# The order of emission of a two-block kernel: 2.4 instead of 1.3 times the estimated latency for the steps of the RWKV7 recurrence

## The chip, the cores and the metric

The kernel runs on one core of a Trainium2 chip. The metric is the device time of one execution in microseconds (us). TensorE (PE), VectorE (DVE), ScalarE (ACT), GpSimd (POOL) and SyncE (SP, which issues the loads of the weights here) run in parallel, each through its own queue in order, and wait for each other by semaphores.

## What is computed

Two blocks run one after the other on one sequence of 256 tokens of width 1024, all in float32. Only the first block (two layers) is touched by the change:

```
for l in range(2):
    h = rmsnorm(x, norm_g[l])
    proj = h @ w_in[l]                          # 1024 x 18688
    y_a = hgrn2_mixer(...) * silu(a_g)          # 8 heads of 128, both directions
    y_b = retention_mixer(...) * silu(b_g)      # 8 heads, value width 256
    y_c = rwkv7_mixer(...) * silu(c_g)          # 16 heads of 64, both directions
    gates = sigmoid(merge)
    x = x + (gates0 * (y_a @ w_branch_a) + gates1 * (y_b @ w_branch_b)
             + gates2 * (y_c @ w_branch_c)) @ w_out
# rwkv7, for each token t and direction:
#   S = S * w_t + (S @ -kk_t) (kk_t * a_t)^T + v_t k_t^T;   o_t = S @ r_t
```

The second block (feed-forward layers, a short convolution, latent attention, attention to a memory) follows and stays as it is.

## The kernel before

Weights come in tiles of 128 x 1024 floats. Each is split into a high and a low part (ScalarE makes `whi`, L411, VectorE makes `wlo`, L412), and each product is made of three matmuls (L370 to L372, in `mm3`). A chunk is 1024 rows by 256 columns of a weight matrix: 16 pieces of three matmuls. The matmuls of a chunk write `pj` (projections), `pg` (gates of the merge), `pb` (branches) or `po` (output).

The work of a layer is written as five Python generators, and `weave` (L39) emits their instructions. Four are chains of dependent steps: `recurrences` (RWKV7: 8 pairs of heads, in chunks of 64 tokens), `heads` (4 pairs of HGRN2 heads, then 4 pairs of retention heads), `outs` and `operands` (before and after each pair of the recurrence). The fifth, `weights`, is the filler: projections, gates and branches, piece by piece. A chain's step yields (cost, latency) in estimated ns, a piece of weights yields 320, and either may yield a function: it is then left alone until the function says yes. `weave` keeps a clock, `now`. It takes the first chain whose due time has come, in the order recurrences, heads, outs, operands; if there is none it takes a piece of weights; and if the weights wait too, it moves the clock on to the next due time. After a step of a chain:

```
now += v[0]
ready[g] = now + scale[g] * v[1]
```

So `scale` (1.3 for recurrences, 1.35, 1.3 and 0.8 for the others) says how many times its estimated latency a step is allowed before the next step of its chain is due. The order of emission is the priority by which the compiler's scheduler orders the instructions of each engine among those that it holds to be ready; within a pool of tiles the buffers go round in the order of emission. `Ahead` (L94) moves the recurrence's instructions on VectorE, ScalarE and GpSimd 50 places up, and the splits of the weights go 80 up.

`recurrences` (L723) runs 9 rounds: `states(p-1)` and `prologue(p)` in step with each other (`in_step`, L69: costs are added, the larger latency counts). `prologue` is `rwkv_scores` (L982): a matmul for the bonus (L1009), scores (`psc`, L1021) into `SCa` and `SCr`, then an inverse by doubling, four times `pw` (L1081) and `px` (L1089) with VectorE work after each, and two last steps. `states` is `rwkv_states` (L1117): 10 steps of four small matmuls (`ch`, L1135, L1142, L1151) and then the outputs (`po`, L1169 and L1176). After it `("s", p)` is set.

The filler's order in `weights` (L746) is: HGRN2's inputs (4 times 5 chunks), retention's first pair (6), four gates of branch 0, a wait for the fourth pair of HGRN2 heads, branch 0 (4), retention's second and third pair (12), four gates of branch 1, branch 1's first half, retention's last pair, branch 1's second half, four gates of branch 2. What may be put in sooner by `spare` (L757) are the recurrence's own inputs k, v, r, g (4 chunks for every two pairs, in `NB` = 4 buffers, so each only when the fourth one before it has been used) and the gates of branch 0. HGRN2's and retention's inputs share a ring of five buffers (`ring`, L657). The gates of branch 1 share the buffers `SCr` with the recurrence's scores, and so they wait:

```
if tasks and (tasks[0][0] == 0 or ("s", 7) in ev):   # in spare
if b > 0:
    yield from until(("s", 7))                       # in gates
```

PSUM holds two banks for the filler's sums (`ps`). After `weave` come branch 2 (from all pairs of the recurrence) and the output projection, in plain order.

Of the kernel before, what the change touches and what calls it, by code (L numbers as in the profile page):

```python
# [29 lines left out]
def run(gen):  # L30

    try:
        while True:
            next(gen)
    except StopIteration as e:
        return e.value


def weave(chains, fill):  # L39

    scale = dict(chains)
    now, ready, wait, live = 0.0, {}, {}, list(scale) + [fill]
    while live:
        free = []
        for g in live:
            if g in wait and wait[g]():
                del wait[g]
                ready[g] = max(now, ready.get(g, 0.0))  # L50
            if g not in wait:
                free.append(g)
        g = next((g for g in free if g is not fill and ready.get(g, 0.0) <= now), None)
        if g is None:
            g = fill if fill in free else min(free, key=lambda g: ready.get(g, 0.0))
        now = max(now, ready.get(g, 0.0))
        v = next(g, None)
        if v is None:
            live.remove(g)
        elif callable(v):  # L60
            wait[g] = v
        elif g is fill:
            now += v
        else:
            now += v[0]
            ready[g] = now + scale[g] * v[1]


def in_step(gens):  # L69

    live, wait = list(gens), {}
    while live:
        took, later, moved = 0.0, 0.0, False
        for g in list(live):
            if g in wait and not wait[g]():
                continue
            wait.pop(g, None)
            v = next(g, None)
            while callable(v) and v():
                v = next(g, None)  # L80
            if v is None:
                live.remove(g)
            elif callable(v):
                wait[g] = v
            else:
                took, later, moved = took + v[0], max(later, v[1]), True
        if moved:
            yield took, later
        elif live:
            stuck = [wait[g] for g in live]  # L90
            yield lambda: any(w() for w in stuck)
# [430 lines left out]
class First(Core):  # L522
# [76 lines left out]
    def layer(s, l, then):  # L599
# [88 lines left out]
        def room():  # L688

            if due:  # L690
                n = 4 * due[0][0] + due[0][1] - NB
                return n < 0 or ("kvrg"[n % 4] + " used", 2 * (n // 4) + 1) in ev
            return True
# [8 lines left out]
        def operands():  # L702
            for p in range(8):
                for n in "kvr":
                    yield after((n, p // 2))
                if p > 0:
                    yield after(("bt", p - 1))
                yield from s.rwkv_operands(l, p, part("r", p), part("k", p), part("v", p), codes, ops)
                ev.add(("o", p))
                ev.add(("k used", p))  # L710
# [3 lines left out]
        def prologue(p):  # L714
            yield after(("o", p))
            pre[p] = yield from s.rwkv_scores(l, p, part("r", p), part("v", p), ops.pop(p), ev,
                                              lambda: p < 2 or ("g used", p - 2) in ev)

        def states(p):
            yield from s.rwkv_states(p, pre.pop(p), sts, lambda: p == 0 or ("g used", p - 1) in ev)  # L720
            ev.add(("s", p))

        def recurrences():  # L723

            for p in range(9):
                yield from in_step([states(p - 1)] * (p > 0) + [prologue(p)] * (p < 8))

        def outs():
            for p in range(8):
                yield after(("s", p))  # L730
                yield after(("g", p // 2))
                yield from s.rwkv_out(l, p, sts.pop(p), part("g", p))
                ev.add(("g used", p))

        def heads():
            st["ys"] = s.hs
            for j in range(4):
                yield lambda: ("h", j) in hin
                yield from s.hgrn_pair(l, j, hin["h", j], st["ys"], ev)
                ev.add(("h", j))  # L740
            for j in range(4):
                new = None if j % 2 else after(("a", ) if j == 0 else ("b", 0))
                yield from s.ret_pair(l, j, hin[("t", j)], st, new, ev)
                ev.add(("t", j))

        def weights():  # L746
            gate = lambda b, j: s.gate(l, b, j, st)

            def hproj(j):
                yield from s.hgrn_in(l, j, pj, pt, ring, hin)  # L750

            def rproj(j):
                yield from s.ret_in(l, j, pj, pt, ring, hin)

            tasks = [(b, gate(b, j)) for b in range(2) for j in range(4)]

            def spare():  # L757

                if due and room():
                    yield from rkv(*due.pop(0))  # L760
                    return True
                if tasks and (tasks[0][0] == 0 or ("s", 7) in ev):
                    yield from tasks.pop(0)[1]
                    return True
                return False

            def gates(b):
                if b > 0:
                    yield from until(("s", 7))
                while tasks and tasks[0][0] <= b:  # L770
                    yield from tasks.pop(0)[1]

            def until(*e):
                for i in e:
                    while i not in ev:
                        if not (yield from spare()):
                            yield after(i)

            def filled(g):

                for v in g:
                    while callable(v) and not v():
                        if not (yield from spare()):
                            yield v
                    if not callable(v):
                        yield v

            for j in range(4):
                yield from filled(hproj(j))
            yield from filled(rproj(0))  # L790
            yield from gates(0)
            yield from until(("h", 3))
            for j in range(4):
                yield from s.branch(l, 0, j, s.chunk(s.a["wba"][l][j]), st["ys"], st)
            ev.add(("a", ))
            yield from filled(rproj(1))
            yield from filled(rproj(2))
            yield from gates(1)
            for half in range(2):
                if half == 1:  # L800
                    yield from filled(rproj(3))
                yield from until(("t", 2 * half))
                for j in (0, 2):
                    b = [s.branch(l, 1, i, s.chunk(s.a["wbb"][l][i][2 * half:2 * half + 2]), st["ys"], st, True)
                         for i in (j, j + 1)]
                    for i in b:
                        for _ in range(8):
                            yield next(i)
                    yield after(("t", 2 * half + 1))
                    for i in b:  # L810
                        yield from i
                ev.add(("b", half))
            for j in range(4):
                yield from gate(2, j)
            while due:
                yield room
                yield from rkv(*due.pop(0))
# [15 lines left out]
        s.normed(s.x, y, s.P(f"ng{l}"), s.hb)  # L833
        if l == 0:
            nc.sync.dma_start(out=s.c1, in_=s.a["c1"])
        weave(((recurrences(), 1.3), (heads(), 1.35), (outs(), 1.3), (operands(), 0.8)), weights())
        run(out_c(0))
        run(out_c(1))
        mixed = st["gate", 0]
# [21 lines left out]
    def gate(s, l, b, j, st):  # L861

        if b == j == 0:
            st["gate", 0] = s.xp.tile([128, 8, T], F32, tag="x", name="gate")
        p = s.bank("pg")
        yield from s.fm(p, s.chunk(s.a["win"][l][MERGE + 4 * b + j]), s.hb)
        if b > 0 and j % 2 == 0:
            st["gate", b, j // 2] = s.rp.tile([128, 4, T], F32, tag="SCr", name="gate", bufs=2)
        s.nc.scalar.activation(s.gates(b, j, st), p, AF.Tanh, scale=0.5)
# [1035 lines left out]
```

## Time and profile before

| | us |
|---|---|
| median of 3 runs | 2739.27 (2730.82 to 2743.38) |
| the profiled execution | 2742.64 |
| its span, first to last instruction | 2740.8 |
| PE / DVE / ACT / POOL busy | 2636.6 / 2068.3 / 1494.7 / 283.6 |

The two layers of the first block take about 1690 us of the span: the first from the start to about 862 us, the second, with the same stretches, some 841 us later. Busy time is the time in which an engine worked on something; matmuls are pipelined, so a busy PE isn't PE at its peak. PEclk is the share of the full clock that TensorE was granted: 1.0 is 2.4 GHz, 0.5 is 1.2 GHz, and means lie between.

### The profile page before, as it was taken

How to read it: one execution, taken by the hardware profiler on the slowest of the kernel's cores; microseconds unless marked ns; L12 is line 12 of the kernel's file. 1: busy time of each engine (PE TensorE's matmuls, PEld its weight loads, DVE VectorE, ACT ScalarE, POOL GpSimd, SP SyncE). 2: the span in 40 equal slices, each digit the busy share in tenths (PEclk: the TensorE clock that was granted, in tenths of full speed). 3: DMA queues.
4: the chain of work that ended last, by engine and by line, in shares of the span. 5: the costliest groups of instructions: out<-in, count | busy, mean ns of one | idle time of the engine just before them, and what ended most of it. 6: DMA issues, size and time to landing. Idle time of an engine off the chain costs nothing.

```text
span 2740.8 us, 76128 instructions
## 1 busy us (share of the span) xinstructions
PE 2636.6 (96%) x31971; PEld 2499.4 (91%) x31971; DVE 2068.3 (75%) x4578; ACT 1494.7 (55%) x2968; POOL 283.6 (10%) x385
## 2 busy tenths in 40 slices
PE   7999999999999899999999999999999999999999
PEld 7888888899999888888799999999999999987999
DVE  8988889866668988898967677766776767756665
ACT  6665646444456665656444455555555555554554
POOL 1111112101021222212100111000000000000000
PEclk9998999999999999999999999999999999998999
DMA  5332222244556332223245555556455655542555
GB/s 178 111 105 75 98 76 83 94 150 151 179 171 197 112 106 84 93 80 100 73 133 163 173 165 197 184 171 187 151 181 182 185 180 163 170 132 76 173 182 161
DMA packets 111800, 385.38 MB, mean 141 GB/s; under 512 B 12384, under 2 KB 16992, under 8 KB 111200
## 3 DMA queue, kind: packets, MB, share of 16 engines
q1 hardware_dynamic: 111024, 379.86, 42.9%
q8 instruction: 251, 4.11, 0.6%
q10 hardware_dynamic: 432, 0.64, 0.1%
q14 instruction: 93, 0.76, 0.1%
HBM read 378.36 MB, written 2.10 MB: 139 GB/s over the span
## 4 chain that ended last, share of the span: by engine, by line
PE 76%; DVE 16%; ACT 3%; issue 2%; POOL 1%; DMA 1%; SPq 0%; ACTq 0%; DVEq 0%; POOLq 0%
PE pj L370 7%; PE pj L372 6%; PE pj L371 6%; PE pg L370 4%; PE pg L372 4%; PE pg L371 4%; DVE wlo L412 4%; PE pw L370 3%; PE pw L372 3%; PE pw L371 3%; PE pu L370 3%; PE pu L372 3%; PE pu L371 3%; PE pb L370 2%; PE pb L371 2%; PE pb L372 2%
## 5 line engine op out<-in xcount | busy, mean ns | idle before, releaser
L411 ACT CAST whi<-raw 128x512 fp32r<-128x512 f32 (+1 forms) x1407 | 862.0, 618 | 825.3 <-PE pj L372 228.0
L412 DVE TENSOR_TENSOR wlo<-raw,whi 128x512 fp32r<-128x512 f32 (+1 forms) x1407 | 984.8, 707 | 422.0 <-ACT whi L411 412.4
L370 PE MATMUL pj<-hb,wlo 128*128 128x256 f32 x1408 | 425.3, 302 | 7.5 <-DVE wlo L412 7.1
L372 PE MATMUL pj<-hb,whi 128*128 128x256 f32 x1408 | 405.0, 288 | 0.0
L371 PE MATMUL pj<-hb,whi 128*128 128x256 f32 x1408 | 404.3, 287 | 0.0
L370 PEld LDWEIGHTS pj<-hb,wlo 128*128 128x128 f32 x1408 | 271.4, 193 | 19.5 <-DVE wlo L412 6.7
L371 PEld LDWEIGHTS pj<-hb,whi 128*128 128x128 f32 x1408 | 271.9, 193 | 1.9 <-issue 0.2
L372 PEld LDWEIGHTS pj<-hb,whi 128*128 128x128 f32 x1408 | 271.6, 193 | 1.4 <-issue 0.2
L371 PE MATMUL pg<-hs,whi 128*128 128x256 f32 x704 | 200.3, 284 | 2.0 <-DVE hs L499 2.0
L370 PE MATMUL pg<-hs,wlo 128*128 128x256 f32 x704 | 200.2, 284 | 1.5 <-DVE x L518 1.5
L370 PE MATMUL pu<-hs,wlo 128*128 128x256 f32 x704 | 199.9, 284 | 1.8 <-DVE wlo L412 1.6
L370 PE MATMUL pw<-g,wlo 128*128 128x256 f32 x704 | 199.6, 284 | 0.7 <-DVE wlo L412 0.7
L372 PE MATMUL pg<-hs,whi 128*128 128x256 f32 x704 | 200.2, 284 | 0.0
L372 PE MATMUL pu<-hs,whi 128*128 128x256 f32 x704 | 199.6, 283 | 0.0
L371 PE MATMUL pu<-hs,whi 128*128 128x256 f32 x704 | 199.3, 283 | 0.0
L371 PE MATMUL pw<-g,whi 128*128 128x256 f32 x704 | 199.2, 283 | 0.0
L372 PE MATMUL pw<-g,whi 128*128 128x256 f32 x704 | 199.2, 283 | 0.0
L370 PE MATMUL pb<-hs,wlo 128*128 128x256 f32 x512 | 145.3, 284 | 0.0
L371 PE MATMUL pb<-hs,whi 128*128 128x256 f32 x512 | 144.6, 282 | 0.0
L372 PE MATMUL pb<-hs,whi 128*128 128x256 f32 x512 | 144.6, 282 | 0.0
L371 PEld LDWEIGHTS pg<-hs,whi 128*128 128x128 f32 x704 | 135.7, 193 | 2.2 <-DVE hs L499 2.2
L370 PEld LDWEIGHTS pu<-hs,wlo 128*128 128x128 f32 x704 | 135.0, 192 | 2.6 <-DVE wlo L412 2.4
(526 smaller groups left out, 6852.8 us busy)
## 6 DMA issues: line engine op xcount, KB each, us to landing
raw<-in_win SPq DMA_DIRECT2D x292, 512.0 KB, 3.6
raw<-in_w SPq DMA_DIRECT2D x256, 512.0 KB, 3.6
raw<-in_wbb SPq DMA_DIRECT2D x32, 512.0 KB, 3.6
raw<-in_wo SPq DMA_DIRECT2D x32, 512.0 KB, 3.5
raw<-in_wconv SPq DMA_DIRECT2D x20, 512.0 KB, 3.6
raw<-in_wba SPq DMA_DIRECT2D x16, 512.0 KB, 3.5
raw<-in_wbc SPq DMA_DIRECT2D x16, 512.0 KB, 3.5
raw<-in_lora SPq DMA_DIRECT2D x16, 256.0 KB, 2.6
```

What stands on the lines that cost most here:

```text
L370: mm(out=out, lhsT=al, rhs=bh, start=start, stop=False)
L371: mm(out=out, lhsT=ah, rhs=bl, start=False, stop=False)
L372: mm(out=out, lhsT=ah, rhs=bh, start=False, stop=stop)
L411: s.nc.scalar.copy(dh, src)
L412: (eng or s.nc.vector).tensor_tensor(dl, src, dh.bitcast(F32), ALU.subtract)
```

## The change

In `layer`, the number that goes with `recurrences()` in the call of `weave` becomes 2.4. Each step of the recurrence is then due 2.4 instead of 1.3 times its estimated latency after the one before it, in both layers. No instruction, buffer, wait or size is changed in the source; what changes is the place of instructions in the order of emission.

```diff
-        weave(((recurrences(), 1.3), (heads(), 1.35), (outs(), 1.3), (operands(), 0.8)), weights())
+        weave(((recurrences(), 2.4), (heads(), 1.35), (outs(), 1.3), (operands(), 0.8)), weights())
```

## Rows read from the trace of the kernel before

**Rows 1.** The page: busy time of each engine; the chain that ended last.

```profile
PE 2636.6 (96%) x31971; PEld 2499.4 (91%) x31971; DVE 2068.3 (75%) x4578; ACT 1494.7 (55%) x2968; POOL 283.6 (10%) x385
PE 76%; DVE 16%; ACT 3%; issue 2%; POOL 1%; DMA 1%; SPq 0%; ACTq 0%; DVEq 0%; POOLq 0%
```

**Rows 2.** Table of stretches: first layer's woven part, then two of the second layer.

```profile
core 0: us, PE busy (x) PEld busy (x) DVE busy (x) ACT busy (x) POOL busy (x), PEclk, DMA share, GB/s
46.80:541.00 494.20, 463.12 (x9031) 415.28 (x9030) 431.92 (x1092) 285.49 (x613) 88.29 (x142) 0.96 0.28 91
541.00:570.00 29.00, 29.00 (x283) 25.89 (x282) 15.86 (x42) 10.99 (x25) 0.73 (x1) 0.94 0.33 105
570.00:678.00 108.00, 107.39 (x855) 104.78 (x854) 77.20 (x150) 49.49 (x95) 11.11 (x12) 1.00 0.49 159
678.00:812.00 134.00, 133.76 (x1104) 132.55 (x1103) 89.62 (x144) 67.66 (x123) 19.94 (x14) 1.00 0.54 175
888.00:1383.00 495.00, 463.99 (x9082) 415.72 (x9081) 433.76 (x1102) 297.31 (x642) 100.75 (x150) 0.97 0.29 95
...
1412.00:1520.50 108.50, 107.89 (x866) 105.20 (x862) 76.90 (x149) 49.97 (x96) 10.82 (x12) 1.00 0.50 158
```

**Rows 3.** Waits of PE, 46.8 to 541 us.

```profile
engine line waited for: us in total, times, longest us
PE pw L1081 <- DVE XY L105: 5.3, 4, 2.0
PE pj L370 <- DVE wlo L412: 4.5, 4, 1.7
PE px L1089 <- DVE W L105: 2.8, 2, 1.9
```

**Rows 4.** Marks of order, first layer: duration ns min/median/max, first and last start us.

```profile
L1021 PE MATMUL psc<-ar,bk x256: 272/272/577, 63.6 to 495.1; 64*128 64x128 f32 x128
L1176 PE MATMUL po<-ar,S x192: 218/218/267, 163.6 to 569.3; 64*64 64x64 f32 x192
L470 PE MATMUL hpn<-c,rs x16: 270/272/323, 183.6 to 540.9; 128*128 128x128 f32 x16
L370 PE MATMUL pg<-hb,wlo x64: 277/280/283, 677.9 to 700.2; 128*128 128x256 f32 x64
```

**Rows 5.** PE's groups, 46.8 to 541 us: count | busy us, mean ns | idle before.

```profile
L370 PE MATMUL pj<-hb,wlo 128*128 128x256 f32 x479 | 148.5, 310 | 4.7 <-DVE wlo L412 4.5 <-ACT hb L411 0.2
...
L370 PE MATMUL pj<-whi,hb 128*128 128x256 f32 x95 | 28.7, 302 | 0.6 <-issue 0.6
...
L370 PE MATMUL pg<-hb,wlo 128*128 128x256 f32 x64 | 20.3, 317 | 1.0 <-DVE wlo L412 1.0
...
L1342 PE MATMUL ppt<-Z 128*32 128x32 f32 (+2 forms) x224 | 12.1, 226 | 0.1
...
L1252 PE MATMUL hpo<-P,v 128*128 128x256 f32 x32 | 10.5, 459 | 2.4 <-POOL P L1351 2.4
```

**Rows 6.** Table of stretches: one where the fill runs out, one of four gates' chunks.

```profile
344.90:375.00 30.10, 27.00 (x500) 22.32 (x503) 25.23 (x68) 12.49 (x32) 6.05 (x13) 0.83 0.11 37
...
678.00:701.00 23.00, 23.00 (x198) 23.00 (x197) 13.12 (x20) 12.20 (x21) 1.87 (x2) 1.00 0.56 183
```

**Rows 7.** PE's timeline inside 344.9 to 375 us: start us, us, line, tiles.

```profile
347.44 0.33 PE L1336 MATMUL ppt<-Z 128*32 128x32 f32 x16 [1.25 <-DVE Z L1321]
...
359.81 0.43 PE L1142 MATMUL ch<-RV,X 64*64 64x64 f32 x4
...
363.15 0.45 PE L1151 MATMUL ch<-UV,bT 128*64 128x64 f32 x8
...
366.84 0.69 PE L1135 MATMUL ch<-S,ar 64*64 64x64 f32 x8
...
374.83 0.46 PE L1298 MATMUL ppc<-D,EK 128*32 128x32 f32 x32
```

## The prediction

> **What bounds the kernel now.** I read the page first: engines, slices, chain. TensorE is busy for 96% of the span and carries 76% of the chain that ended last; VectorE carries 16% [rows 1]. An average hides the stages, so next comes the table of stretches [rows 2]. Each of the first two layers' woven parts has two regimes. From 46.8 to 541 us (the four head pairs of HGRN2, seven and a half of the recurrence's eight pairs, 40 chunks of weights) PE is busy for 463.1 of 494.2 us at a mean granted clock of 0.96, and VectorE for 431.9. From 541 to 812 us PE is busy for 29.0 + 107.4 + 133.8 = 270.2 of 271 us, VectorE for 182.7. So the second regime is TensorE alone; the first has 31 us of PE gaps, and stretches at the lower of the clock's two levels (1.2 instead of 2.4 GHz). The second layer's rows are the same to 1 us. The list of waits names the gaps: PE waits for VectorE's steps of the recurrence and for the weight splits [rows 3]. All that the change can win lies in these 31 us and the slow clock, twice.
>
> The reader then needs four marks of order [rows 4]. The recurrence's score matmuls (psc) run from 63.6 to 495.1 us, its last output matmul (po) at 569.3; HGRN2's fourth norm (hpn) is done at 541; the gates of branch 1 (pg) start at 677.9. The last mark matters: the generator of weights doesn't emit those four gates before the last pair's states exist (`until(("s", 7))`). Now 108 us lie between the two.
>
> **The planner's clock, by hand.** The factor only enters `ready[g] = now + scale*latency`, so its effect on the order can be added up from the yields. One step of the recurrence loop is a list of 13 yields: costs 0.48 + 2 x 0.9 + 8 x 0.8 + 0.33 + 0.33 + 0.9 + 2 x 0.4 = 11.0, plus the states of the pair before, 10 x 0.23 + 1.9 = 4.2: 15.2 planned us. Latencies 2.5 + 2 x 1.8 + 4 x (1.5 + 1.8) + 1.3 + 2.0 = 22.6. Each step also waits some 0.25 for the piece under way. A pair takes 15.2 + 1.3 x 22.6 + 3.3 = 48 planned us now, and 15.2 + 2.4 x 22.6 + 3.3 = 73 after: eight pairs 384 or 582, and 20 to 41 for the last states. The trace's pairs are at most (495.1 - 63.6)/7 = 61.6 us apart [rows 4], 1.28 real for one planned.
>
> The heads' factor stays. One head pair of HGRN2 has 56.5 of latency x 1.35, 8.3 of costs and some 4 of waiting: 89 planned, four of them 356, hence the fourth at about 368. Real: (540.9 - 183.6)/3 = 119 us [rows 4].
>
> What is emitted in such a period of 89? Before: 9.6 chunks of 16 pieces of 0.32 (49), 1.85 pairs of the recurrence (28), the heads' 8.3 and 3 for operands and outs: 89, no room left. The 40 chunks to 541 us, (479 + 95 + 64)/16 [rows 5], agree: 20 for HGRN2, 4 gates, 4 of retention's, and the recurrence's own k, v, r, g, which the generator loads only as older ones are used up. After: 1.22 pairs (18.6), and the slower recurrence also frees only 7 of its 12 chunks by then, so 35 chunks in all, 8.4 per period (43); 8.3 and 2: 72 of 89. **17 planned us of each period have nothing in them.** No other chunk can be moved in: HGRN2's and retention's wait for the ring of five buffers, branch 0 for the fourth head, gates of branch 1 for the last states.
>
> **The change part by part.** No instruction is added or removed; some 2.5 pairs (7.4 by 541 us now, 4.9 after) and 5 chunks move from the first regime to the second.
>
> 1. The first regime gets shorter. Its 72 planned us of work at the present rate, 119/89, are 96 real. What the 17 empty ones cost is not in the trace as such; the nearest row is the one place where fill runs out now, 344.9 to 375 us [rows 6]. There HGRN2 goes from ppt (347.4) to the next head's ppc (374.8) in 27.4 us [rows 7], for which the plan (three levels, P, the sum, D, all times 1.35) has 27; PE is busy, partly at the low clock (0.83), and a single chunk fits. So a starved chain gains nothing on its plan while the recurrence beside it is dense; without that, 1/1.35 of it is a floor. Bounds for the period: 463.1/4.15 = 112 us of PE busy now, less 1.2 chunks x 5.75 us [rows 6] and 0.63 pair x 24 (below) = 90 us if PE never stood still, and 96 + 17 = 113. I take 103, 7 of the 17, because the recurrence's steps in the dry stretch are thinner than in [rows 7]. 4.15 periods (494/119): -66 us.
>
> 2. The second regime gets longer, since PE has no gap there [rows 2]: every matmul moved in is paid in full. A chunk is 23.0/4 = 5.75 us [rows 6]. A pair: PE's 463.1 us less 39.9 x 5.75 = 229 and some 40 for the heads (ppt 12.1, hpo 10.5 and smaller ones [rows 5]) leave 194 for 7.7 pairs, 25, of which a twentieth is slow clock: 24. 2.5 x 24 + 5 x 5.75 = +89 us. Their VectorE and ScalarE work is hidden: VectorE is busy 71% from 570 to 678 us.
>
> 3. A new wait. At the fourth head (planned 368) 4.9 pairs are done. What is left to emit ahead of the gates of branch 1 is 23 chunks (2 + 12 of retention, 4 of branch 0, 5 of the recurrence), 118 planned, and 26 of retention heads and operands; with the recurrence's share of 15.2 in 73 that lasts (118 + 26)/0.79 = 182, in which 2.5 more pairs go. So fill ends at pair 7.4, and 8 steps of the last pair and 11 of its states come bare. What queues behind the wait: all of the layer's remaining weights, the four gates first, then branch 1 and retention's last pair, and with them SP's loads for them. Bare steps are seen at 359.8, 363.2 and 366.8 us, some 3.5 apart, with the slow clock [rows 6, 7]; with nothing else to do I take 2.6: 19 x 2.6 = 49 us, of which PE works 15. Two PSUM banks let the next two gates' matmuls run ahead, four if the slot of the sixth pair's scores (SCr) is free: 12 to 23 us of cover. +4 to +33 us; I take +10, near full cover. The SCr slots, the ring, and the lora loads on SP move with their pairs and cost nothing of their own: SP's queue waits for buffers, and DMA is 28 to 54% busy.
>
> Sum per layer: -66 + 89 + 10 = +33 us, twice +66. The profiled execution took 2742.64 us (span 2740.8), 3.4 above the median of the runs: 2808.6 there, **2805 us** on the median, 2.4% slower.
>
> **The rivals.** (a) Balance wins. The first regime has VectorE busy 87% and PE 94%, the second VectorE 67%; taking VectorE work out could end PE's waits. Price: a period of 94 us (90 is PE's floor), -104 + 89 + 4 = -11 per layer, 2717 us; at the floor with no bare steps -31 per layer, 2677. For it: the waits are on VectorE [rows 3]. Against it: fill is lacking in 17 of 89. It decides from a period of 95. The Trainium skill says the same as this rival in "Perfetto Trace Analysis", section Optimization Strategy: where the most-contended engine changes over time, interleave the regimes. By that rule the time falls; it doesn't ask whether there is work left to interleave with, which is what I count here.
>
> (b) Nothing moves: PE's matmuls are conserved, the first part gives back what the second takes (period 97, good cover), 2739. That also holds if the compiler's scheduler, which takes what is ready, reorders the change away: then the last po stays near 569 us.
>
> (c) Head chain as the bound. If HGRN2's chain keeps about the plan's pace in the dry stretches (period 113) and the bare end is not covered: -25 + 89 + 33 = +97 per layer, 2933. With the 119 of now it would be over 2970, which I hold for very unlikely, as VectorE has less to do.
>
> **How the numbers follow.** Forecast (2760 to 2880) 0.57; (a) 0.18; (b) 0.13; (c) 0.12. The range drops the lowest part of (a) and the upper part of (c): 2715 to 2900. A measurement of this kernel can tell about 0.5%, 14 us, from no change. Faster by more 0.18, same 0.13, slower 0.69.
>
> **What would show it.** hpn's fourth norm at about 475 us instead of 541 (step 1; 515 speaks for (c), under 440 for (a)); five fewer chunks before it; PE busy under 90% and more low-clock stretches from 47 us to there. The last po near 750 us instead of 569, and the gates of branch 1 at or after it, with PE gaps of some us between its ch steps (step 3). A po that ends before the gates' matmuls with PE solid throughout would prove step 3 wrong; a first regime with PE at 97% would prove the whole forecast wrong.

## The result, and the profile after

The changed kernel takes 2752.96 us, median of 8 runs (2748.61 to 2761.12); the kernel before, beside it on the same chip, 2737.92 us (2722.16 to 2750.26, 8 runs). The ratio is 1.0053, with a 95% interval of 1.003 to 1.0076: slower by some 15 us. The forecast was 2805. The time lies inside the range of 2715 to 2900 and on the forecast side, but less than a quarter of the forecast loss of 66 us came, and it is below the 2760 to 2880 that the forecast gave itself.

The page of the changed kernel: busy time of each engine, then PE, DVE and the granted clock in the 40 slices of the span (2746.9 us, against 2740.8).

```profile
PE 2635.4 (96%) x31971; PEld 2498.1 (91%) x31971; DVE 2069.7 (75%) x4578; ACT 1494.4 (54%) x2968; POOL 285.3 (10%) x385
PE   7999989999999999999999999999999999999999
DVE  8889888776678978988777677766776667666765
PEclk9999989999999999998999999999999999998999
```

Every engine has worked as long as before [rows 1]. What moved shows only by stretch. I cut each layer where HGRN2's fourth norm ends: the first regime from the start of the weave to it, the second from it to the end of the gates of branch 2. First the two regimes of the first layer before (the stretches of [rows 2] cut at other places), columns as in [rows 2].

```profile
42.40:540.90 498.50, 466.43 (x9050) 417.83 (x9048) 436.17 (x1103) 288.64 (x621) 88.29 (x142) 0.96 0.29 92
540.90:811.60 270.70, 269.85 (x2236) 262.84 (x2235) 182.54 (x334) 128.04 (x241) 31.79 (x26) 0.99 0.50 161
```

The same two in the second layer before:

```profile
892.80:1383.90 491.10, 460.09 (x9049) 411.65 (x9047) 430.58 (x1094) 294.89 (x637) 100.75 (x150) 0.97 0.29 93
1383.90:1654.70 270.80, 269.94 (x2236) 263.11 (x2236) 181.80 (x334) 128.05 (x241) 31.77 (x26) 0.99 0.50 161
```

The two regimes after, in the first layer and then in the second:

```profile
43.20:450.40 407.20, 377.38 (x6568) 342.33 (x6567) 359.17 (x887) 242.36 (x505) 77.82 (x122) 0.95 0.30 99
450.40:811.90 361.50, 357.29 (x4717) 337.42 (x4717) 257.94 (x550) 173.49 (x357) 43.56 (x46) 1.00 0.43 136
893.80:1304.70 410.90, 377.12 (x6568) 341.70 (x6566) 357.34 (x879) 249.94 (x521) 89.67 (x130) 0.95 0.30 98
1304.70:1665.60 360.90, 357.05 (x4717) 337.31 (x4716) 257.57 (x550) 173.45 (x357) 43.25 (x46) 1.00 0.42 137
```

In the first layer the first regime is 91.3 us shorter and the second 90.8 longer, so it comes out even, 769.2 and 768.7. In both kernels PE stands still in the first regime for some 30 us (498.5 - 466.4 = 32.1 and 407.2 - 377.4 = 29.8), and spends an estimated 40 us of it at the lower level of the clock (twice the share missing from the rounded PEclk: 2 x 0.04 x 498.5 = 40 and 2 x 0.05 x 407.2 = 41). VectorE is busy for 0.875 of it before and 0.882 after. The second layer went from 761.9 to 771.8 in these executions, with PE's gaps in it going from 31.9 to 37.7 us. The spans of these two executions differ by 6 us and the medians of the runs by 15; one execution each doesn't place the rest.

The marks of order, for [rows 4]: the whole span for the first two lines, then 40 to 460 us and 600 to 760 us.

```profile
L1021 PE MATMUL psc<-ar,bk x256: 272/272/373, 64.6 to 614.3; 64*128 64x128 f32 x128
L1176 PE MATMUL po<-ar,S x192: 218/218/267, 207.8 to 686.4; 64*64 64x64 f32 x192
L470 PE MATMUL hpn<-c,rs x16: 270/273/322, 179.7 to 450.1; 128*128 128x128 f32 x16
L370 PE MATMUL pg<-hb,wlo x64: 276/282/387, 665.0 to 700.2; 128*128 128x256 f32 x64
```

HGRN2's fourth norm is at 450 us instead of 541, the last product with the state at 686 instead of 569, and the gates of branch 1 start at 665, before the recurrence has ended. The next row is the end of the recurrence, where the prediction had put bare steps. PE is solid there:

```profile
664.70:690.70 26.00, 25.99 (x324) 22.23 (x324) 13.67 (x45) 10.68 (x26) 0.73 (x1) 1.00 0.22 70
```

PE's waits from 46 to 450 us (columns as in [rows 3]) have a new first line. Before, this wait came to 2.4 us in the first regime [rows 5].

```profile
PE hpo L1252 <- POOL P L1351: 10.2, 5, 3.4
PE pw L1081 <- DVE XY L105: 3.4, 3, 1.5
PE pk L478 <- DVE wide L455: 3.0, 5, 0.9
```

One of the stretches behind it, as a row of the table:

```profile
395.00:414.00 19.00, 14.22 (x384) 11.74 (x382) 16.82 (x36) 6.17 (x13) 6.72 (x10) 0.64 0.09 30
```

And PE's timeline in it (in brackets the idle time ahead of an instruction, and what ended it):

```profile
401.15 2.07 PE L1252 MATMUL hpo<-P,v 128*128 128x256 f32 x4 [2.92 <-POOL P L1351]
407.43 1.08 PE L1089 MATMUL px<-XY,W 32*32 32x32 f32 x64 [1.31 <-DVE W L105]
```

So the dry stretches that the prediction expected, in which little of the filler is at hand, are there (PE busy 14.2 of 19 us, clock 0.64, DMA 9%). VectorE, though, is busy for 16.8 of these 19 us: while PE lacks work, VectorE doesn't.

### The profile page after: what moved, and what is told of

It is laid out like the page before. It is cut to its first block, busy times and chain, and to the rows that moved or that the text cites. A ratio compares the mean times of both kernels' runs of the same rounds, so it can differ in the third digit from the quotient of the medians.

```text
span 2746.9 us, 76204 instructions
## 1 busy us (share of the span) xinstructions
PE 2635.4 (96%) x31971; PEld 2498.1 (91%) x31971; DVE 2069.7 (75%) x4578; ACT 1494.4 (54%) x2968; POOL 285.3 (10%) x385
## 4 chain that ended last, share of the span: by engine, by line
PE 50%; DVE 5%; ACT 1%; issue 1%; DMA 0%; POOL 0%; ACTq 0%; DVEq 0%; POOLq 0%
PE pg L370 3%; PE pg L372 3%; PE pg L371 3%; PE pw L370 3%; PE pw L372 3%; PE pw L371 3%; PE pu L370 3%; PE pu L372 3%; PE pu L371 3%; PE pj L370 2%; PE pj L371 2%; PE pj L372 2%; DVE wlo L412 1%; PE pb L370 1%; PE pb L371 1%; PE pb L372 1%
## 5 line engine op out<-in xcount | busy, mean ns | idle before, releaser
L370 PE MATMUL pj<-hb,wlo 128*128 128x256 f32 x1408 | 422.8, 301 | 3.8 <-DVE wlo L412 3.1
L371 PE MATMUL pj<-hb,whi 128*128 128x256 f32 x1408 | 408.8, 290 | 0.1
L370 PEld LDWEIGHTS pj<-hb,wlo 128*128 128x128 f32 x1408 | 274.5, 195 | 12.8 <-DVE wlo L412 4.3
L371 PEld LDWEIGHTS pj<-hb,whi 128*128 128x128 f32 x1408 | 275.0, 195 | 2.5 <-DVE hb L412 0.5
L372 PEld LDWEIGHTS pj<-hb,whi 128*128 128x128 f32 x1408 | 274.9, 195 | 1.5
L370 PE MATMUL pg<-hs,wlo 128*128 128x256 f32 x704 | 200.0, 284 | 2.2 <-DVE x L518 2.2
L371 PE MATMUL pg<-hs,whi 128*128 128x256 f32 x704 | 200.1, 284 | 2.0 <-DVE hs L499 2.0
L370 PE MATMUL pu<-hs,wlo 128*128 128x256 f32 x704 | 199.8, 284 | 1.6 <-DVE wlo L412 1.6
L370 PE MATMUL pw<-g,wlo 128*128 128x256 f32 x704 | 199.6, 284 | 0.7 <-DVE wlo L412 0.7
L371 PE MATMUL pu<-hs,whi 128*128 128x256 f32 x704 | 199.3, 283 | 0.0
L371 PE MATMUL pw<-g,whi 128*128 128x256 f32 x704 | 199.2, 283 | 0.0
L370 PE MATMUL pb<-hs,wlo 128*128 128x256 f32 x512 | 146.2, 285 | 0.0
L371 PE MATMUL pb<-hs,whi 128*128 128x256 f32 x512 | 144.6, 282 | 0.0
L370 PEld LDWEIGHTS pg<-hs,wlo 128*128 128x128 f32 x704 | 135.6, 193 | 2.4 <-issue 2.4
L371 PEld LDWEIGHTS pg<-hs,whi 128*128 128x128 f32 x704 | 135.6, 193 | 2.2 <-DVE hs L499 2.2
```

The source lines that it names most:

```text
L370: mm(out=out, lhsT=al, rhs=bh, start=start, stop=False)
L371: mm(out=out, lhsT=ah, rhs=bl, start=False, stop=False)
L372: mm(out=out, lhsT=ah, rhs=bh, start=False, stop=stop)
```

## The experiments

The letters in the expectations are names of theories; each expectation says what its theory holds. All ratios are to the kernel before.

**Other factors for the recurrence.** The edit is one number; 1.8, 2.0, 2.2 and 2.6 were run beside the change's 2.4.

```diff
-        weave(((recurrences(), 1.3), (heads(), 1.35), (outs(), 1.3), (operands(), 0.8)), weights())
+        weave(((recurrences(), 2.0), (heads(), 1.35), (outs(), 1.3), (operands(), 0.8)), weights())
```

> Recurrence factor 1.8, halfway. Theory W (work is conserved: a layer costs PE's work plus some 32 us of gaps, whatever the factor, since gaps only change their owner): within 0.3% of before, ratio 1.000 to 1.003, fourth hpn of the first layer near 500 us, gates 812 us. Rival E (the planner's empty time costs): by hand a pair is 15.2 + 1.8 x 22.6 + 3.3 = 59 planned us, 80 of a period's 89 are filled, so about half of what 2.4 cost: ratio 1.0025. Rival B (the cost at 2.4 is the bare end of the recurrence): at 1.8 the recurrence ends before the fill does, so 1.000.

> Recurrence factor 2.0. By hand a pair is 15.2 + 2.0 x 22.6 + 3.3 = 64 planned us; the recurrence ends at 13 + 512 + 33 = 558, about where the fill ahead of the gates ends. Theory V with the trade it implies (moving work of v us of VectorE and p of PE from the first to the second regime changes a layer by p - v/0.88): between 1.8 and 2.4, ratio 0.993 to 1.003. Rival (1.8 was an accident of one order): at or above 1.003.

> Recurrence allowed 2.2 times its latency, nothing else changed. Theory D (VectorE sets the first regime; what is moved pays while PE's work going into the second regime is less than VectorE's work leaving the first, divided by its busy share; past that the first regime is left with too few chunks for HGRN2's heads and waits of its own appear): 0.995 to 1.000, between 0.992 at 2.0 and 1.005 at 2.4, with the sum per layer 756 to 764 us. Rival N (2.4 hit one unlucky order; there is no turn): 0.992 or less.

> Recurrence allowed 2.6 times its latency. Theory D: the turn goes on, 1.006 to 1.020, fourth state product of the first layer at 445 us or earlier but by less than 12 us, last product with the state later than 686. Rival N: below 1.003, since 2.4 was the unlucky one.

| factor | median us | ratio (95%) | first layer: first + second regime | PE gaps in the first, us | PE's wait for L1351, both layers, us |
|---|---|---|---|---|---|
| 1.3 | 2737.07 to 2739.96 beside the others | 1 | 498.5 + 270.7 = 769.2 | 32.1 | 4.7 |
| 1.8 | 2723.55 | 0.9929 [0.9904, 0.9954] | 436.6 + 321.2 = 757.8 | 27.1 | 10.3 |
| 2.0 | 2717.64 | 0.9919 [0.9893, 0.9946] | 412.9 + 336.6 = 749.5 | 21.8 | 11.4 |
| 2.2 | 2737.54 | 0.9998 [0.9979, 1.0017] | 418.9 + 346.7 = 765.6 | 27.3 | 20.2 |
| 2.4 | 2752.96 | 1.0053 [1.003, 1.0076] | 407.2 + 361.5 = 768.7 | 29.8 | 21.5 |
| 2.6 | 2745.33 | 1.0025 [1.0009, 1.0041] | 396.5 + 369.2 = 765.7 | 30.7 | 11.3 |

The last three columns are of one execution each; that of 2.2 took 2747.33 us, 10 above its median, the others stand within 5 us of theirs.

None of the three theories of the expectation for 1.8 allowed a gain, and 0.7% was gained. 2.0 came at the favourable edge of what was expected, and 2.2 inside it, with the first layer at 765.6 us, just above the expected 764.

The kernel with 2.0 beats both 1.3 and 2.4. Its first regimes in the two layers, with the second regime of the first layer between them:

```profile
42.80:455.70 412.90, 391.15 (x7264) 353.66 (x7263) 371.57 (x937) 258.02 (x542) 84.20 (x129) 0.97 0.32 99
455.70:792.30 336.60, 335.00 (x4022) 319.47 (x4021) 241.36 (x500) 159.36 (x324) 38.14 (x39) 1.00 0.46 144
872.70:1290.00 417.30, 394.56 (x7264) 356.67 (x7262) 370.94 (x929) 268.50 (x560) 90.74 (x137) 0.96 0.32 98
```

VectorE is busy for 0.90 and 0.89 of the first regime, PE's gaps are 21.8 and 22.7 us. From 2.0 to 2.4 the first layer loses 19.2 us, and the rows of both regimes account for it: PE's gaps went from 21.8 + 1.6 to 29.8 + 4.2 us (+10.6), and PE's busy time from 391.2 + 335.0 to 377.4 + 357.3 (+8.5). The matmuls are the same, and the granted clock fell from 0.97 to 0.95. The turn lies between 2.0 and 2.2. It isn't smooth: theory D wanted 1.006 or more at 2.6, and 1.0025 lies where rival N had it (though N's other claim, that there is no turn, fell with 2.2). 2.2 has more chunks in its first regime than 2.0 (37.2 against 36.2, by the count of L370's pieces). What a factor gives is thus a turn of 0.8% between 2.0 and 2.2, and a scatter of about half a per cent from order to order beyond it.

**One layer alone.** The factor 2.4 in one layer, 1.3 in the other.

```diff
+        weave(((recurrences(), 2.4 if l == 0 else 1.3), (heads(), 1.35), (outs(), 1.3), (operands(), 0.8)), weights())
```

> Factor 2.4 in the first layer only, 1.3 in the second. In the profiled execution the first layer came out even (gates done at 811.5 us in both) and the second 10.8 us later. If that difference is a property of the layers: this kernel within 3 us of before, ratio 0.999 to 1.001. If it was one execution's accident and each layer pays half: +7 us, ratio 1.0026.

> Factor 2.4 in the second layer only. If the second layer alone pays: +10 to +14 us, ratio 1.004 to 1.005. If each layer pays half: +7 us, ratio 1.0026.

0.9999 [0.998, 1.0018] for the first layer alone (2740.91 us), 1.0031 [1.0015, 1.0047] for the second alone (2747.68). The loss shows in the second layer alone, as in the traces above; it is small, so there is no single large cost in either. These two traces give a second reading of each layer, from the start of the weave to the end of the gates: at 1.3 765.6 and 763.2 us (first and second layer; 769.2 and 761.9 above), at 2.4 767.7 and 767.8 (768.7 and 771.8 above). So a layer scatters by some 4 us from one execution to the next, and how the loss divides between the layers is only roughly known.

**Whose work sets the first regime.** The prediction took PE for it. Three kernels keep the order of before and make one engine's work lighter, a fourth does it with the order of the change. They leave arithmetic out, and are compared by their stretches alone, one execution each. Without the matmul of L371, PE is busy for 7% less in the first regime:

```diff
 def mm3(...)
-        mm(out=out, lhsT=ah, rhs=bl, start=False, stop=False)
```

Without the subtraction that makes `wlo` VectorE has 23% less (`hi` stands in for `lo`; the lines that make the tiles and hand them out are left out here):

```diff
-                s.split(hi, lo, part)
+                s.nc.scalar.copy(hi, part)
```

> Before's order, and one of the three matmuls of each piece left out everywhere (L371, the high part of the weights times the low part of the activations): a chunk on PE falls from 5.75 to some 3.85 us, and all of VectorE's and ScalarE's work stays. In the first regime of a layer that takes 40 x 1.9 = 76 us from PE's 463. If PE's work bounds the first regime (W): it falls from 494 to about 420 to 430 us. If VectorE (432 busy of 494) is what holds it: to no less than 455 to 460. The second regime should fall by 40 x 1.9 = 76 us in both.

> Before's order; left out: only the low part of each weight tile (VectorE's 120 us of the first regime's 432), all matmuls stay. Theory V: PE's 463 us now bound the first regime, its gaps shrink from 31 to some 10 us, fourth hpn at 505 to 525 us. Rival L (latency of the chains): 535 to 541. Rival P (PE's own work was the bound): 530 to 541 as well, with the waits for VectorE's split (some 6 us) gone.

> Before's order; left out: the low part of each weight tile (VectorE's subtraction L412 for weights; the high part is used in its place) and the matmul L371. Of the first regime's work that takes some 120 us from VectorE's 432 and 76 from PE's 463; the recurrence and the heads stay whole. Leaving out L371 alone left the fourth hpn at 540 us. Theory V (VectorE's work bounds the first regime, at 88% busy): now PE's remaining 390 us or VectorE's 310 bound it, and the fourth hpn comes at 420 to 460 us. Rival L (the chains' own latency bounds it): hpn stays above 500 us.

> The changed order (2.4), and L371 left out everywhere, as was tried with before's order. PE loses some 68 us of the first regime's 377. Theory V: VectorE's 358 us at 88% busy still bound it, fourth hpn within 8 us of the changed kernel's 450. Rival P: near 390 us. The second regime loses 45 x 1.9 = 86 us.

The first regime of the first layer in each, columns as in [rows 2]. Order of before, without L371:

```profile
37.40:540.80 503.40, 432.88 (x8449) 371.17 (x8447) 441.53 (x1115) 288.98 (x631) 90.06 (x143) 0.87 0.30 92
```

Order of before, without the subtraction:

```profile
41.70:509.20 467.50, 446.44 (x9052) 402.93 (x9050) 337.62 (x934) 290.17 (x625) 77.60 (x143) 0.98 0.31 97
```

Order of before, without either:

```profile
34.60:459.40 424.80, 389.02 (x8411) 339.50 (x8411) 336.54 (x937) 284.57 (x626) 79.16 (x142) 0.95 0.35 110
```

Order of the change (2.4), without L371:

```profile
37.70:440.30 402.60, 339.43 (x6030) 294.35 (x6032) 358.96 (x896) 240.12 (x509) 81.56 (x122) 0.88 0.32 102
```

With PE's busy time down from 466 to 433 us, the regime didn't get shorter at all: 503.4 us, VectorE still busy for 0.877 of it, and PE's gaps grew from 32 to 70 us. The work left out was more than these 33 us: 40 chunks at 1.9 us are 76, by the expectation's estimate; the granted clock was 0.87 instead of 0.96. The same at 2.4: 402.6 against 407.2, VectorE at 0.892. With VectorE's work down by 98.6 us the regime is 31 us shorter, and then PE fills 446 of 467.5 us and is the next bound. (PE's waits for `wlo`, which go with the subtraction, were 7.4 us before, so they don't make up the 31.) With both lighter it is 424.8, which also shows that no chain's latency held it at 500. So in the order of before VectorE's work sets the first regime, at a busy share of about 0.88, with PE's work close behind. At 2.4 these runs show only that PE's work doesn't set it: VectorE was not made lighter there.

Most of the expectations of theory V held. Three numbers were missed: PE's gaps without the subtraction (21 us, some 10 expected), the fourth norm at 2.4 without L371 (440 us, 442 to 458 expected), and the second regime. That one was to lose 76 and 86 us, and lost 44.5 and 60.3 (270.7 to 226.2 and 361.5 to 301.2), because without L371 PE is no longer solid in it. Its rows, in the order of before and in that of the change:

```profile
540.80:767.00 226.20, 201.55 (x1552) 191.66 (x1551) 173.01 (x326) 119.68 (x230) 32.09 (x25) 0.95 0.62 188
440.30:741.50 301.20, 284.47 (x3976) 259.24 (x3975) 249.62 (x544) 165.99 (x352) 44.15 (x46) 0.97 0.51 160
```

The whole runs took 2492.02, 2663.44, 2138.07 and 2443.64 us. The last of them against the first is worth a look: without L371, the order of the change is worth -48 us instead of +15 (one execution each).

**Additions of HGRN2 on VectorE.** The new wait names the additions of L1351 on GpSimd; they are put on VectorE, at 2.4, 1.8 and 1.3.

```diff
-            nc.gpsimd.tensor_tensor(dst, dst, cm[...], ALU.add)
+            tt(dst, dst, cm[...], ALU.add)
```

> Factor 2.4, and the four small additions at the end of each HGRN2 head (L1351, into P) on VectorE instead of GpSimd. At 2.4 PE waits 21.5 us in all for these (9.7 us before the change). Theory D (the gaps of the first regime now belong to HGRN2's own chain in dry stretches, and this link is its longest): the wait shrinks to a third and the kernel is 8 to 14 us faster than the changed one, ratio to before 0.999 to 1.002. Rival: the next link of the chain takes over and nothing changes, 1.004 to 1.006; rival: VectorE, busy 88% there, is the bound, and 64 more instructions on it make it slower, over 1.006.

> Factor 1.8 and the additions into P (L1351) on VectorE. At 1.8 PE waits 10.3 us in all for these. Theory D (the gaps belong to HGRN2's own chain where the fill is thin): some 6 to 10 us faster than 1.8 alone, ratio to before 0.989 to 0.992. Rival (VectorE is near its bound, so what is put on it is paid): no gain over 1.8 alone, 0.993 or more.

> Factor 1.3 as before, the additions into P on VectorE. Theory D says that the wait for P grows only where the fill is thin; here it is 4.8 us in all (two of 2.4), so 0 to 5 us are won, ratio 0.998 to 1.000. Rival (the additions on GpSimd are slow at any factor, and the 20 us won at 2.4 have nothing to do with the factor): 15 to 20 us won here too, 0.993.

At 2.4: 2732.95 us, 0.9982 [0.9965, 0.9999], 0.7% less than the changed kernel. At 1.8: 2727.95, 0.9953 [0.9937, 0.997], no gain over 1.8 alone (0.9929). At 1.3: 2730.47, 0.9967 [0.9952, 0.9982]. PE's wait for the additions fell from 21.5 to 2.8 us at 2.4 and from 10.3 to 0.4 at 1.8. (The 9.7 us for the kernel before in the first of these expectations adds the waits of the weight loads; PE's own are 4.7.) It is tempting to say that the new wait cost 2.4 most of what it lost. That isn't shown: at 1.8 the wait went too and nothing was gained, and at 1.3, where there was hardly such a wait, 0.3% was, more than theory D's 0.2%. It is not the reason why 1.8 and 2.0 are better. VectorE is fuller for it (363.2 of 400.2 us at 2.4, a share of 0.908): with 4 us more work on VectorE the first layer's first regime is 7 us shorter (the second layer's 6, 410.9 to 404.9). So at 2.4 VectorE's work alone doesn't set its length, and 0.88 isn't the most that VectorE can do in it; links of HGRN2's chain seem to cost some us there.

**HGRN2's heads, further apart or closer.** At 2.4 for the recurrence, with 1.9 or 1.2 for the heads.

```diff
+        weave(((recurrences(), 2.4), (heads(), 1.2), (outs(), 1.3), (operands(), 0.8)), weights())
```

> Recurrence 2.4, heads 1.9 instead of 1.35 times their latency. By hand a head pair's period is then 56.5 x 1.9 + 12 = 120 planned us, with 1.64 pairs of the recurrence (25), some 9.4 chunks (48) and 11 for the rest: 36 of 120 are empty, twice what the change left (17 of 89). Theory E (empty planner time costs real time, 7 of 17 as the prediction had it): 30 us per layer slower than the changed kernel, ratio to before 1.02 to 1.03. Theory W (what is empty in the plan takes no time on the chip; the steps just follow each other as soon as they can): within 10 us of the changed kernel or below it, ratio 0.995 to 1.008.

> The changed kernel's 2.4 for the recurrence, and HGRN2's heads at 1.2 instead of their factor, so that their steps stand closer to one another and less of the first regime is empty by the plan. If the dry stretches of the changed kernel come of empty planned time: 1.002 or less, gaps of PE in the first regime under 27 us. Theory D with the waits for POOL as the new bound: heads that stand closer wait more for each other's sums, 1.005 or more, gaps 30 us or more.

With 1.9 the ratio is 1.0093 [1.0062, 1.0124] (2765.74 us), with 1.2 it is 0.9987 [0.9969, 1.0005] (2735.83). The first regimes of both layers with 1.2:

```profile
42.80:431.00 388.20, 361.94 (x6402) 327.12 (x6401) 352.92 (x861) 237.61 (x499) 77.77 (x121) 0.97 0.33 102
882.50:1276.60 394.10, 366.53 (x6402) 331.98 (x6401) 348.13 (x852) 244.21 (x515) 86.12 (x129) 0.95 0.33 101
```

Gaps are 26.3 and 27.6 us instead of 29.8 and 33.8 (under 27 was expected if empty planned time is the cause), VectorE's shares 0.91 and 0.88. Three factors for the heads, 1.2, 1.35 and 1.9, stand at 0.9987, 1.0053 and 1.0093, which agrees with planned time costing something when nothing is in it; the three orders differ in more than that, so it isn't shown. It costs little in any case: with 1.9 nearly the whole of the longer plan came back as more chunks and pairs in the first regime (477.4 us against 407.2, 294.2 against 361.5 in the second). The expectation of 1.02 to 1.03 for empty planned time falls, and its rival's 0.995 to 1.008 was just exceeded.

The period of a head pair, a third of the time from the first of the four hpn norms to the last in the first layer, doesn't follow the plan: 87.4 us where 80 are planned (1.2), 90.1 for 89 (1.35), 108.1 for 120 (1.9).

## Why the prediction was right or wrong

**The bound that was read, wrong.** "PE 94%, VectorE 87%" was read as PE with waits. The stretch without L371 shows the opposite: PE's busy time down by 7%, nothing gained. A busy share of 0.88 on VectorE was already close to the most that any run here shows in this mix; in the first layer it kept between 0.87 and 0.90 with every factor of the table, while its work in the regime fell from 436 to 352 us, and 0.91 was the highest of all these runs. The rows of before held a hint: PE's weight loads were busy for 417.8 of 498.5 us, 84%, less than VectorE's 87%. The Trainium skill, "Perfetto Trace Analysis", section Identifying the Most-Contended Engine, says that the matmuls' busy share is not a good measure of how near TensorE is to its peak, and names the busy share of the weight loads as one of two better ones; by that share VectorE comes first in this regime, and the runs without L371 agree.

**The planner's clock, right.** 4.9 pairs were forecast by the fourth head: psc's last start is 614.3, so pairs are (614.3 - 64.6)/7 = 78.5 us apart, and (450.1 - 64.6)/78.5 = 4.9. The chunks before the fourth head are down from 39.9 to 35.8, where 35 were forecast.

**Step 1, the first regime: this is the step that failed.** It forecast -66 us, with a period of 103 and the fourth norm at 475. The period was (450.1 - 179.7)/3 = 90.1, where [rows 4] gave 119, and the regime got 91.3 us shorter in the first layer and 80.2 in the second (491.1 to 410.9). In the second layer the period went from 115.9 to 91.5. Two terms were wrong, in opposite directions. The larger is the length of a period: the 72 planned us of work were held at the old rate of 119/89, which makes 96, and 7 empty us were added. But the rate was no property of the plan. 119 was the time that VectorE took for a period's work in the order of before, and it has 77.0 us less of it in the regime (436.2 to 359.2): at a share of 0.88 that is 77/0.88 = 87.5 us of time, near the 91.3 that went. That the period then fell on the planned 89 doesn't make the plan its bound, as with the heads' other factors it lies 7 us above the plan or 12 below it. The 17 empty us show as the dry stretches, and there PE loses again what it lost before in waits. PE's busy time fell by 89 us, as counted (22 a period by 4.15: 91); the forecast amounts to gaps that grow from 31 to some 56 us, and they stayed at 30. PE stayed busy for 93% of the regime, where under 90% was the sign to look for. The smaller error is the count of 4.15 periods: only the three between the norms got shorter (by 87 us together); the part up to the first norm went from 183.6 - 42.4 = 141.2 to 179.7 - 43.2 = 136.5. With the right period and 4.15 of them it would have been -120.

That the two layers differ, -0.5 and +9.9 us, lies mostly in the kernel before. The prediction read its layers as the same to 1 us from windows of nearly the same length; cut at its own marks, the second layer's first regime is 491.1 us, 7.4 shorter than the first's, and had less to give. Part of that is scatter: in the two traces with one layer changed, the first regimes at 1.3 take 494.9 and 493.9 us.

**Step 2, the second regime, right.** +89 forecast, +90.8 and +90.1 measured (270.7 to 361.5, and 270.8 to 360.9), PE solid in it at full clock (357.3 of 361.5, 1.00). Of the 90.8, 87.4 are busy time of PE and 3.3 are gaps; 4.25 chunks moved instead of 5 (4 us less) and the gaps came on top, so that the fit is this close is partly luck. VectorE's share there, 257.9 of 361.5 = 0.71, left room.

**Step 3, the bare end, in the right place and wrong in size.** +10 forecast (4 to 33); the gates of branch 1 began at 665.0, 21 us before the last po, and the end of the recurrence has PE at 25.99 of 26.0 us. The gates' matmuls ran ahead and filled it: 38 of each of the three lines lie in these 26 us. PE's gaps in the whole second regime went from 0.9 to 4.2 us, nearly all of it ahead of the gates. The last po came at 686, where 750 was expected.

**The sum.** +33 per layer became -0.5 and +9.9: step 1 by -25 and -14 us, step 3 by -10, and step 2 by +2 and +1, in which the gaps ahead of the gates are contained.

**The rivals.** By size it went as (b), nothing moves, and for its reason: PE's matmuls are conserved and the first regime gave back what the second took. The rest of it didn't come: its period was 97, and po moved by 117 us, so the change was not reordered away. Rival (a) names the right mechanism, VectorE's work going out of the regime that it bounds; its period came below the 95 from which it was to decide (90.1), and yet the time didn't fall, since only three periods got shorter: 89 + 4 us by 3 is 31 a period, so the point lay at 88. In "Perfetto Trace Analysis", section Optimization Strategy, the Trainium skill says that interleaving regimes with different most-contended engines may improve the time; here that holds at 1.8 and 2.0 (0.9929 and 0.9919) and no longer at 2.2 and above (0.9998 to 1.0053). Rival (c), the heads' chain as the bound with a period of 113, did not come: it was 90.1. That this chain holds back a few us at 2.4 is not excluded, as the additions on VectorE show.

**Why so little moves, and which way.** What is moved counts twice: its VectorE time leaves a regime that VectorE bounds, and is worth itself divided by 0.88; its PE time enters one that PE bounds, and costs itself. At 2.4 that is 77.0/0.88 = 87.5 against 87.4 us of PE (269.9 to 357.3): even. At 1.8, 2.0, 2.2 and 2.6 the same sum gives a first layer shorter by 5, 8, 2 and 0 us; the table has it shorter by 11, 20, 4 and 4. So the trade is close to even, leans to a gain at 1.8 and 2.0, and accounts for less than half of what came there. Without L371, 82.6/0.88 = 94 us should leave the first regime (VectorE's 441.5 to 359.0), and 100.8 did; PE brings 82.9 us into the second (201.6 to 284.5), which grows by only 75.0, because there PE had gaps to fill (24.7 us, then 16.7). So the change gains, as measured.

In the kernel as it is, what is left beside the trade is how well the first regime is packed: PE's gaps and slow clock in it, those 31 us and the slow clock that the prediction had called all that can be won. At 2.0 a third of the gaps goes; at 2.4 they are back, with the wait for GpSimd's additions and the dry stretches in the place of the waits of [rows 3].

What stays open: why the packing turns between 2.0 and 2.2. The wait for L1351 nearly doubles at this very place, from 11.4 to 20.2 us over both layers, but it isn't enough: at 2.6 it is 11.3 again and the kernel stays slower than at 2.0, and taking the wait out at 1.8 gained nothing. Empty planned time isn't enough either, as it grows with the factor while 2.6 is no slower than 2.4. Whether VectorE's work or a chain sets the first regime at 2.4 was not tried by making VectorE lighter in that order.

## What to carry to other kernels

Before costing a move between two stretches, find out for each which engine it pays in: take some of one engine's work out and see whether the stretch gets shorter, because an engine at a share of 0.88 can be the one that sets the stretch while another stands at 0.94. Moved work is then worth about its time on the first stretch's engine (divided by that engine's usual share) less its time on the second's, and where the two are about even, look for the gain in the packing and try several amounts: 2.0 gained 0.8% where 2.4 lost 0.5%. This planner's estimates gave the order and the amounts well, but not the rate, which went with the load of the engine that was the bound.

## What the runs showed of the hardware

GpSimd's additions of 32 x 64 elements (L1351) had twice the median duration in the changed kernel (668 ns) that they had before (317). First the line of before, then that of after (duration ns min/median/max, first and last start us).

```profile
L1351 POOL TENSOR_TENSOR P<-P,cm x64: 306/317/742, 117.5 to 1371.9; 32x64 f32<-32x64 f32 x64
```

```profile
L1351 POOL TENSOR_TENSOR P<-P,cm x64: 310/668/847, 116.2 to 1291.7; 32x64 f32<-32x64 f32 x64
```

The dry stretch shows four of them taking 2.68 us while VectorE runs operations of two tensors back to back; the timelines of VectorE and GpSimd there, after:

```profile
398.42 2.68 POOL L1351 TENSOR_TENSOR P<-P,cm 32x64 f32<-32x64 f32 x4
...
398.66 0.80 DVE L965 SCALAR_TENSOR_TENSOR bt<-sg,nkk 128x512 f32<-128x512 f32 x1
399.38 0.80 DVE L973 TENSOR_TENSOR bk<-bk,enL 128x512 f32<-128x512 f32 x1
400.11 0.80 DVE L971 SCALAR_TENSOR_TENSOR bk<-bt,enL 128x512 f32<-128x512 f32 x1
```

With 1.8, 2.0, 2.2 and 2.6 the medians are 405, 382, 362 and 558 ns; moved to VectorE, at 2.4, the same additions have a median of 216 ns. The Trainium skill, "Perfetto Trace Analysis", section Optimizing Scalar/DVE Operations, says that GpSimd's read port is shared with VectorE, so that shifting work between those two might not help. The durations here agree with a shared port but no run isolates it, and what the shift was worth depended on the order: 0.7% at 2.4, 0.3% at 1.3, nothing at 1.8.

The second thing is the clock that TensorE was granted in the first regime of the first layer, beside PE's gaps there: 0.87 with 70.5 us of gaps in 503.4 (without L371), 0.88 with 63.2 in 402.6 (the same at 2.4), 0.96 with 32.1 in 498.5 (before), 0.98 with 21.1 in 467.5 (VectorE lighter). In the first of these, PE's busy time is only 33.6 us less than before, where the matmuls left out were worth an estimated 76.
